# A two-layer trunk kernel: more seven-product pairs in layer 0, sums made by transfers, late loads on GpSimd's queue

## The chip, the cores and the metric

The kernel runs on one core of a Trainium2 chip. The metric is device time in microseconds (us) of one execution. A profiled execution gives the trace, in which the time of each instruction on each engine is recorded: TensorE (PE; its weight loads are PEld), VectorE (DVE), ScalarE (ACT), GpSimd (POOL) and SyncE (SP), which issues most transfers.

## What is computed

One step of a decoder of two layers for a prompt of 512 tokens and 8 samples of 8 tokens, 576 columns in all, model width 1024, inner width 2048:

```python
x = x + short_conv_mixer(rmsnorm(x))   # layer 0
x = x + mlstm_mixer(rmsnorm(x))        # layer 1, 4 heads of 512
y = rmsnorm(x)

def short_conv_mixer(h, buf, w_in, conv_w, w_out):
    b_gate, c_gate, xa, z = jnp.split(h @ w_in, 4, axis=-1)
    u = c_gate * xa
    conv, new_buf = causal_dwconv(u, buf, conv_w)
    y = b_gate * conv * jax.nn.silu(z)
    return y @ w_out, new_buf

def mlstm_mixer(...):
    xm, z = jnp.split(h @ w_in, 2, axis=-1)
    xc, new_buf = causal_dwconv(xm, conv_buf, conv_w)
    xc = jax.nn.silu(xc + conv_b)
    q, k, v = xc @ w_q, xc @ w_k, xm @ w_v
    ...   # gates, chunkwise matrix memory with state C, n, m for prompt and samples
    out = (norm(h) * onorm_w + skip * xc) * jax.nn.silu(z)
    return out @ w_out, new_buf, C, n, m
```

Everything is float32. A product of float32 matrices is made of three matmuls of rounded parts: high by high, high by low, low by high.

## The kernel before

**Tiles.** Tokens lie along the free axis (576 columns, two halves HT of 288), features along the 128 partitions. A weight chunk is 1024 x 128, loaded as one 512 KB tile `wr` of eight blocks of 128 x 128. There are four such raw buffers. ScalarE casts half a chunk (128x512) to the high part `wh` (L214, L263), VectorE subtracts for the low part `wl` (L215, L264). High and low parts have four buffers each.

**Layer 0** runs over f = 0 to 15 (L590 on). Each f needs the four chunks 4f to 4f+3: c, xa, z and b. A pair of chunks can be done in two ways. The plain one is two calls of `products` (L234), each 8 blocks x 3 parts x 2 column ranges (256 and 320). The other is `block_pair`: the chunks' eight blocks each are seen as a 2 x 2 block matrix, even blocks of the first chunk a11, odd ones a12, those of the second chunk a21 and a22, and the product with the 2 x 2 form of the activations is made from seven products in place of eight, each of four blocks x three parts on 288 columns (L332). The price is sums of weight blocks, made by VectorE: s1 = a21 + a22 (L297), s2 = s1 + a11 (L298), and inside the pair s2 += a12 and a21 += a11 (both L337). The pair's results are combined on ScalarE and VectorE (L342 to L384).

The pair (c, xa) of f+1 is done this way in every turn from f = 1 on. The pair (z, b) of f is done this way only if f is in `SECOND`, before the change 3, 5, 7, 9, 11 and 13. `block_weights` (L301) loads a pair's two chunks and makes s1 and s2 ahead of time, while the pair before is multiplied. s1, s2 and the pair's scratch `pu` are tiles of `X`, which has seven buffers; from f = 11 on c and xa lie there too. A copy of two columns per f is made by GpSimd (L602).

**Layer 1** has its input products in a loop over f (L684 on), where `xm` of some f is multiplied by VectorE straight out of PSUM and of others copied by ScalarE first. Then q and k of each (head h, tile dt) are made by pairs; `spread` (L742 to L748) repeats columns of k in a tile `kd`, which TensorE transposes (`tb`, L756).

**The late part** goes head by head and sample by sample. State tiles are loaded (c<-cs, L177), updated (c, L1222), stored (cs_out<-c, L1191). Values and keys of the prompt, written to memory earlier, come back by `fetch` (L1128): `kss` and `kps` keys, `vps` and `vss` values, `xcs`, `x1s` and `far`, all issued on SP's queue. Key stacks are scaled on ScalarE (L1122). The norm of a head needs `ln`: columns copied by GpSimd (L1315), VectorE's sums, a power on GpSimd (L1323), and VectorE again. `ns` (L1162) is a small sum on GpSimd per head stage.

**Order.** The program is written in one piece and a scheduler orders each engine's instructions by its own estimate of their times. An engine runs its instructions in that order, and an instruction whose input is late holds back all behind it on its engine. SP's transfers wait in the same way: for a free buffer, for data to store, or for a store whose buffer is to be loaded again.

Of the kernel before, what the change touches and what calls it, by code (L numbers as in the profile page):

```python
# [12 lines left out]
ALU = mybir.AluOpType  # L13
# [3 lines left out]
P = 128  # L17
# [3 lines left out]
NW = W // P  # L21
# [34 lines left out]
LAG = 6  # L56
AHEAD = 2
FH = 2
SECOND = tuple(range(3, 14, 2))
FI = 1  # L60
EARLY = 3.45
NEARLY = 10
# [5 lines left out]
def trunk(tc, io):  # L68
    nc = tc.nc
    ctx = ExitStack()  # L70
    with ctx:
# [34 lines left out]
        layer0 = [False]  # L106
# [37 lines left out]
        load = nc.sync.dma_start  # L144
        store = nc.sync.dma_start
        store_act = nc.scalar.dma_start

        cols = const.tile([P, NCOL], F32, name="cols")
        cst = const.tile([P, NCST], F32, name="cst")
# [150 lines left out]

        def block_weights(c1, c2, six=False):  # L301

            groups, behind = [], []
            for i in range(1 + six):
                r1, r2 = weight_tile(), weight_tile()
                for r, c_ in ((r1, c1 + i), (r2, c2 + i)):
                    latest[0] = load(out=r, in_=io["wts"][c_]).ins
                groups.append(block_sums(r1, r2, (8, 4)[i]))
                behind = [r1, r2] if i else []
            ahead_of[c1, c2] = groups, behind  # L310

        def block_pair(c1, c2, fs, xs, out1, out2, add, mid=None, then=None, pops=0, groups=None,
# [24 lines left out]
                    tt(g[out], g[out], g[block_], ALU.add)  # L337

            bx = block("p1")
            product(bx, a11, "b11", True)  # L340
            by = block("p6")
            nc.scalar.activation(by, bx, AF.Copy, scale=-1.0)  # L342
# [7 lines left out]
            nc.scalar.copy(u, by)  # L350
            add_up(s2, a12)
            product(bx, a12, "b21", False)
            add_up(a21, a11)
            run(pops)
            if pops:
                drip()
# [324 lines left out]
        for f in range(NW):  # L681
            if f % 4 == 0:
                ext = T(352, name="ext")
                load(out=ext, in_=io["exb"][f // 4])  # L684
            ext_f = ext[:, 88 * (f % 4):88 * (f % 4) + 88].rearrange("p (b t) -> p b t", t=11)
            if f < 2:
                u = raws[f]
                nc.vector.tensor_tensor(u, u, rb, ALU.mult)
            else:
                acc = gemm(80 + f, 1, h2)  # L690
                u = T(name="xm")
                if 3 < f < NW - 2:
                    nc.vector.tensor_tensor(u, flat(acc), rb, ALU.mult)
                else:
                    nc.scalar.copy(u, flat(acc))
                    nc.vector.tensor_tensor(u, u, rb, ALU.mult)
            us.append(u)
            if f >= 8:
                xm.append(split(u))
            elif f % 2:  # L700
                fm.append(forms(us[f - 1], u))

            cv = []

            def begin(f=f, u=u, ext_f=ext_f, cv=cv):
                cv.append(T(name="xc"))
                cv.extend(conv_steps(cv[0], u, ext_f, [col(f"cb{j}", f) for j in range(4)]))
                cv[1]()

            def end(f=f, u=u, ext=ext, cv=cv):  # L710
                nc.gpsimd.tensor_copy(cpb[:, f, :], u[:, NP - 3:NP])
                nc.scalar.activation(cv[0], cv[0], AF.Silu, bias=col("cbias", f))
                store_act(out=xcs[f], in_=cv[0])
                if f % 4 == 3:
                    store(out=io["exb_out"][f // 4], in_=ext)
                if f == NW - 1:
                    store(out=io["cpb_out"], in_=cpb)

            slow.extend([begin] + [lambda s=s, cv=cv: cv[s]() for s in (2, 3, 4)] + [end])
            if f >= LAG:  # L720
                for _ in range(5):
                    drip()
            if f == NW - 3:
                block_weights(96, 98)
# [14 lines left out]
                else:  # L739
                    nc.vector.tensor_tensor(gacc[:, a:b], g[:, 0:b - a], gacc[:, a:b], ALU.add)  # L740

        def spread(t, dup):  # L742

            for u in range(2):
                nc.gpsimd.tensor_copy(
                    dup[:, 128 * u:128 * u + 128].rearrange("p (g s t) -> p g s t", g=4, s=4),
                    t[:, NP + 32 * u:NP + 32 * u + 32].rearrange("p (g t) -> p g t", t=8)
                    .unsqueeze(2).broadcast_to([P, 4, 4, 8]))  # L748
# [155 lines left out]
        for h in (3, 0, 1, 2):  # L904
            st = heads[h]
            for dt in range(4):
                f = 4 * h + dt
                k, q = T(name="k"), T(name="q")

                def next_stage():  # L910
                    for m in range(KD):
                        x = T(name="x")
                        load(out=x, in_=x1s[m])
                        xs.append(x)
                    run(len(work))
                    second_norm(range(KD))

                if (h, dt) == (2, 3):
                    xs = []
                then = next(((128 + 4 * g, 130 + 4 * g, True) for i, g in enumerate(order) if i and order[i - 1] == f), None)  # L920
                if (h, dt) == (3, 0):
                    gemm_first(128 + 4 * f, 130 + 4 * f, fc, xc, k, q, [lambda j=j: mixed_load(j) for j in (4, 5)], then)
                else:
                    gemm_pair(128 + 4 * f, 130 + 4 * f, fc, xc[4:], k, q, mid=[next_stage] if (h, dt) == (2, 3) else None, then=then, pops=1)
                st["kt"].append(k)
                if dt % 2 == 0:
                    st["kd"].append(T(512, name="kd"))
                dup = st["kd"][-1][:, 256 * (dt % 2):256 * (dt % 2) + 256]
                spread(k, dup)
                if (h, dt) == (3, 0):  # L930
                    work.extend([lambda: None] * 2)
                work.append(lambda k=k, dup=dup, h=h, dt=dt: by_token(
                    k, dup, KSCALE, kps[h][dt].rearrange("p (i d) -> p i d", d=128),
                    kss[h][:, :, 128 * dt:128 * dt + 128]))
                last_q = last_act[0]
                st["qt"].append(q)
                if dt % 2 == 0:
                    qpt = T(512, name="qp")
                    nc.gpsimd.memset(qpt, 0.0)
                    st["qp"].append(qpt.rearrange("p (d x) -> p d x", d=2))  # L940
                query_norm(st, dt, q)
                for u in range(2):
                    nc.gpsimd.tensor_copy(
                        st["qp"][-1][:, dt % 2, 128 * u:128 * u + 128].rearrange("p (g x) -> p g x", x=32)[:, :, 8 * u:8 * u + 8],
                        q[:, NP + 32 * u:NP + 32 * u + 32].rearrange("p (g t) -> p g t", t=8))
# [182 lines left out]
        def fetch(name, *srcs, n=512):  # L1128

            fetched[name] = []  # L1130
            for src in srcs:
                t = T(n, name="ld")
                load(out=t, in_=src)
                fetched[name].append(t)

        def fetch_values(h):
# [473 lines left out]
def _arrays(a):  # L1610
# [5 lines left out]
    kq = np.stack([_chunks(f["b_w_k"][0]), _chunks(f["b_w_q"][0])], 1)  # L1616
    wts = np.concatenate([t.reshape(-1, P, KD, P) for t in (
        ain, _chunks(f["a_w_out"][0]), bin_[:NW], _chunks(f["b_w_v"][0]), kq, bin_[NW:], _chunks(f["b_w_out"][0]))], 0)
    cols = np.zeros((P, NCOL), np.float32)

    def put(name, v):
# [80 lines left out]
```

## Time and profile before

| | us |
|---|---|
| median of three runs (lowest, highest) | 1684.31 (1682.43, 1685.41) |
| the profiled execution | 1682.5 |
| its span, first to last instruction | 1680.7 |
| TensorE busy (matmuls) | 1648.2, 98% |
| VectorE busy | 1121.4, 67% |
| ScalarE busy | 781.2, 46% |
| GpSimd busy | 107.9, 6% |
| moved by transfers, mean | 166 GB/s |

The span is what the trace covers; the time of the execution is a little longer. Busy time of an engine leaves out what it issues and waits for. The granted clock of TensorE, 1.00 at full speed (2.4 GHz) and 0.50 at half (1.2 GHz), has a mean of 0.99.

### The profile page before, as it was taken

What the parts mean: (1) busy time and instruction counts of PE and PEld (TensorE: products, weight loads), DVE (VectorE), ACT (ScalarE), POOL (GpSimd) and SP (SyncE); (2) the same over time, 40 slices, a digit from 0 to 9 for tenths busy, and PEclk for the clock granted to TensorE, in tenths of its full rate; (3) what the DMA queues carried; (4) which work ended last, traced back from release to release, by engine and by line L of the source; (5) the groups of instructions that cost most, each with busy time, mean ns of one, the idle gap of its engine ahead of it and who ended that gap; (6) DMA issues with size and microseconds to landing.
All of it is one profiled execution on the core that took longest, in us unless ns stands there. A gap on an engine that the chain in (4) does not pass through costs nothing. (4 is left out here: it accounts for less than half of the span.)

```text
span 1680.7 us, 31096 instructions
## 1 busy us (share of the span) xinstructions
PE 1648.2 (98%) x12161; PEld 1569.9 (93%) x12161; DVE 1121.4 (67%) x2108; ACT 781.2 (46%) x1548; POOL 107.9 (6%) x241
## 2 busy tenths in 40 slices
PE   9999999999999999999899999999999998998998
PEld 9999999999999999999899989998988787988998
DVE  7988888874336975556856456456468567687775
ACT  5555555543224554535544334344345456555421
POOL 0000000000000000000211010101002000000000
PEclk9999999999999999999999999999999899999999
DMA  5233223333432434535434554453655687997982
GB/s 197 73 96 93 96 88 105 92 104 125 128 114 91 145 116 137 170 116 161 143 107 145 156 183 151 154 182 126 200 184 212 203 275 249 336 341 280 369 305 105
DMA packets 109794, 279.57 MB, mean 166 GB/s; under 512 B 11312, under 2 KB 33712, under 8 KB 109648
## 3 DMA queue, kind: packets, MB, share of 16 engines
q1 hardware_dynamic: 94288, 260.27, 47.2%
q10 hardware_dynamic: 15360, 17.32, 3.0%
q8 instruction: 95, 1.56, 0.4%
q14 instruction: 51, 0.42, 0.1%
HBM read 213.89 MB, written 63.66 MB: 165 GB/s over the span
## 5 line engine op out<-in xcount | busy, mean ns | idle before, releaser
L332 PE MATMUL p<-hi,wh 128*128 128x288 f32 x1316 | 389.3, 297 | 2.1 <-ACT p L342 1.5
L332 PE MATMUL p<-lo,wh 128*128 128x288 f32 x1316 | 387.6, 295 | 0.0
L332 PE MATMUL p<-hi,wl 128*128 128x288 f32 x1316 | 386.7, 295 | 0.0
L234 PE MATMUL acc<-hi,wh 128*128 128x256 f32 (+1 forms) x1328 | 288.9, 299 | 6.2 <-ACT num L1288 5.0
L234 PE MATMUL acc<-lo,wh 128*128 128x256 f32 (+1 forms) x1328 | 288.4, 297 | 0.0
L234 PE MATMUL acc<-hi,wl 128*128 128x256 f32 (+1 forms) x1328 | 287.1, 297 | 0.0
L332 PEld LDWEIGHTS p<-hi,wh 128*128 128x128 f32 x1316 | 247.3, 188 | 10.4 <-DVE ws L337 4.1
L263 ACT CAST wh<-wr 128x256 fp32r<-128x256 f32 (+1 forms) x266 | 152.0, 572 | 225.0 <-PE p L332 120.6
L332 PEld LDWEIGHTS p<-lo,wh 128*128 128x128 f32 x1316 | 247.7, 188 | 0.0
L332 PEld LDWEIGHTS p<-hi,wl 128*128 128x128 f32 x1316 | 247.0, 188 | 0.0
L214 ACT CAST wh<-wr 128x512 fp32r<-128x512 f32 x202 | 124.8, 620 | 239.3 <-PE acc L234 181.0
L234 PEld LDWEIGHTS acc<-hi,wh 128*128 128x128 f32 x1328 | 224.1, 190 | 11.7 <-ACT num L1288 5.2
L264 DVE TENSOR_TENSOR wl<-wr,wh 128x256 fp32r<-128x256 f32 (+1 forms) x266 | 163.1, 627 | 96.2 <-ACT wh L263 94.2
L234 PEld LDWEIGHTS acc<-hi,wl 128*128 128x128 f32 x1328 | 223.7, 190 | 1.5 <-issue 1.3
L234 PEld LDWEIGHTS acc<-lo,wh 128*128 128x128 f32 x1328 | 224.1, 190 | 0.5 <-issue 0.2
L215 DVE TENSOR_TENSOR wl<-wr,wh 128x512 fp32r<-128x512 f32 x202 | 138.7, 688 | 110.7 <-ACT wh L214 102.5
L263 ACT CAST wh<-ws 128x512 fp32r<-128x512 f32 (+1 forms) x177 | 99.9, 566 | 208.6 <-PE p L332 120.7
L264 DVE TENSOR_TENSOR wl<-ws,wh 128x512 fp32r<-128x512 f32 (+1 forms) x177 | 108.7, 620 | 57.6 <-ACT wh L263 57.5
L1222 DVE SCALAR_TENSOR_TENSOR c<-c,cols,r 128x512 f32<-128x512 f32 x128 | 91.3, 739 | 31.6 <-PE r L1221 26.2
L417 PE MATMUL p<-hi,wh 128*128 128x288 f32 x496 | 109.2, 300 | 0.0
L417 PE MATMUL p<-hi,wl 128*128 128x288 f32 x496 | 107.3, 295 | 0.0
L417 PE MATMUL p<-lo,wh 128*128 128x288 f32 x496 | 107.0, 295 | 0.0
(382 smaller groups left out, 2572.8 us busy)
## 6 DMA issues: line engine op xcount, KB each, us to landing
wr<-wts SPq DMA_DIRECT2D x222, 512.0 KB, 3.6
c<-cs SPq DMA_DIRECT2D x112, 512.0 KB, 5.9
cs_out<-c SPq DMA_DIRECT2D x64, 512.0 KB, 6.4
x<-xcs SPq DMA_DIRECT2D x20, 288.0 KB, 4.7
x<-xT SPq DMA_DIRECT2D x16, 288.0 KB, 4.2
xcs<-xc ACTq DMA_DIRECT2D x16, 288.0 KB, 2.5
ld<-xcs SPq DMA_DIRECT2D x16, 288.0 KB, 8.1
cp_out<-cp ACTq DMA_DIRECT2D x16, 257.0 KB, 7.0
```

The lines of the kernel that those rows point to most:

```text
L214: last_act[0] = nc.scalar.copy(hi, raw[:, 4 * i:4 * i + 4, :]).ins
L215: nc.vector.tensor_tensor(lo, raw[:, 4 * i:4 * i + 4, :], hi.bitcast(F32), ALU.subtract)
L234: nc.tensor.matmul(acc[:, o:o + j - i], a[:, k % 4, :], x[:, i:j], start=(first and k == 0 and p == 0), stop=(last and k == 7 and p == 2))
L263: last_act[0] = nc.scalar.copy(hi, src).ins
L264: nc.vector.tensor_tensor(lo, src, hi.bitcast(F32), ALU.subtract)
L332: nc.tensor.matmul(bank_, a[:, j, :], x, start=(start and n + j + i == 0), stop=(n == len(groups) - 1 and j == len(g) - 1 and i == 2), ski ...
L417: nc.tensor.matmul(b, a[:, k % 4, :], x[:, t:t + HT], start=bool(start) and k == 0 and i == 0, stop=(k == n - 1 and i == 2), skip_group_ch ...
L1222: ins = nc.vector.scalar_tensor_tensor(ct[:, j, :], ct[:, j, :], dec[:, o + j:o + j + 1], r, ALU.mult, ALU.add).ins
```

## The change

Five things change.

1. `SECOND` becomes 2 to 14: thirteen second pairs by seven products, six before.
2. In layer 0 the weights of the chunks that go by `block_pair` are written on the host with their even blocks first, so that a11, a12, a21 and a22 are contiguous halves. `block_weights` loads the two chunks, loads one half of the second chunk once more into s1, and issues two adding transfers on GpSimd's queue: the other half of that chunk onto s1, and the first half of the first chunk onto a21. VectorE makes s2 = s1 + a11 at the start of the pair and s2 += a12 inside it.
3. In layer 1 the product `xm` of f = 3 is multiplied by VectorE straight from PSUM.
4. The `spread` copies for (h, dt) = (3, 0) are made by ScalarE in place of GpSimd, and two empty items in the list of work are gone.
5. `fetch` issues on GpSimd's queue.

```diff
-SECOND = tuple(range(3, 14, 2))
+SECOND = tuple(range(2, 15))
...
+        add_load = nc.gpsimd.dma_start
...
         def block_weights(c1, c2, six=False):
 
+            if layer0[0]:
+
+                r1, r2 = weight_tile(), weight_tile()
+                for r, c_ in ((r1, c1), (r2, c2)):
+                    latest[0] = load(out=r, in_=io["wts"][c_]).ins
+                a11, a12, a21, a22 = [r[:, i:i + 4, :] for r in (r1, r2) for i in (0, 4)]
+                s1, s2 = [X(512, name="ws").rearrange("p (k x) -> p k x", x=P) for _ in range(2)]
+                load(out=s1, in_=io["wts"][c2][:, 0:4, :])
+                add_load(out=s1, in_=io["wts"][c2][:, 4:8, :], accum_op=ALU.add)
+                add_load(out=a21, in_=io["wts"][c1][:, 0:4, :], accum_op=ALU.add)
+                ahead_of[c1, c2] = [(a11, a12, a21, a22, s1, s2)], []
+                return
...
             bx = block("p1")
+            if layer0[0]:
+                tt(groups[0][s2], groups[0][s1], groups[0][a11], ALU.add)
             product(bx, a11, "b11", True)
...
-            add_up(a21, a11)
+            if not layer0[0]:
+                add_up(a21, a11)
...
-                if 3 < f < NW - 2:
+                if 2 < f < NW - 2:
                     nc.vector.tensor_tensor(u, flat(acc), rb, ALU.mult)
...
-        def spread(t, dup):
+        def spread(t, dup, copy=nc.gpsimd.tensor_copy):
...
-                nc.gpsimd.tensor_copy(
+                copy(
...
-                spread(k, dup)
-                if (h, dt) == (3, 0):
-                    work.extend([lambda: None] * 2)
+                spread(k, dup, *[nc.scalar.copy] * ((h, dt) == (3, 0)))
...
-                load(out=t, in_=src)
+                nc.gpsimd.dma_start(out=t, in_=src)
...
+    blk = [c for c in range(8, 64) if c % 4 < 2 or c // 4 in SECOND]
+    wts[blk] = wts[blk][:, :, [0, 2, 4, 6, 1, 3, 5, 7]]
```

How this moves instructions is shown at three places; lines of the changed kernel are 16 or so higher than those of the kernel before (L264 is L265 there, L337 is L350, L1133 is L1147, L1315 is L1329, L1323 is L1337). A row is line, operation, output and inputs with their buffers' numbers, and the tile's size.

VectorE in layer 0, over the second half of a pair: before, the next pair's sums stand among the splits `wl` of this one.

```order
L264 TENSOR_TENSOR wl_1862<-ws_1699,wh_1861 128x512
L297 TENSOR_TENSOR ws_1832<-wr_1829 128x512
L298 TENSOR_TENSOR ws_1833<-ws_1832,wr_1828 128x512
L337 TENSOR_TENSOR wr_1829<-wr_1829,wr_1828 128x4x128
L264 TENSOR_TENSOR wl_1882<-ws_1700,wh_1881 128x512
L337 TENSOR_TENSOR ws_1700<-ws_1700,wr_1695 128x512
```

In the changed kernel a whole pair reads so.

```order
L350 TENSOR_TENSOR ws_2025<-ws_2024,wr_2020 128x512
L265 TENSOR_TENSOR wl_2242<-wr_2020,wh_2241 128x512
L660 TENSOR_TENSOR z_2029<-z_2029,rb_470 128x576
L265 TENSOR_TENSOR wl_2260<-wr_2021,wh_2259 128x512
L662 TENSOR_TENSOR cv_1871<-b_2030,cv_1871 128x576
L265 TENSOR_TENSOR wl_2277<-ws_2025,wh_2276 128x512
L663 TENSOR_TENSOR cv_1871<-cv_1871,z_2029 128x576
L354 TENSOR_TENSOR ws_2173<-ws_2172,wr_2168 128x512
```

Two of four sums are left, and s2 of the next pair (L354) stands ahead of this pair's last split.

GpSimd in layer 0: before, one copy of two columns per f.

```order
L602 COPY cpa<-u_1550 128x2
L602 COPY cpa<-u_1826 128x2
L602 COPY cpa<-u_2120 128x2
L602 COPY cpa<-u_2396 128x2
L602 COPY cpa<-u_2693 128x2
```

After, the adding transfers stand between the copies, two for each pair, 27 pairs in all.

```order
L312 DMA ws_1728<-wts 128x512
L618 COPY cpa<-u_1574 128x2
L313 DMA wr_1725<-wts 128x512
L312 DMA ws_1876<-wts 128x512
L313 DMA wr_1873<-wts 128x512
L312 DMA ws_2024<-wts 128x512
L618 COPY cpa<-u_1870 128x2
L313 DMA wr_2021<-wts 128x512
```

The copies keep their order, and each now stands behind transfers that wait for the chunk or for the first half of s1.

GpSimd in the late part, from the norm of one head (copy of `qc`, power) to the next head's first copies: before, nothing stands between.

```order
L1315 COPY ln_18067<-qc_16793 128x1
L1323 TENSOR_TENSOR ln_18067<-ln_18067,half 128x5
L1162 TENSOR_TENSOR ns_19285<-nst,cols_15623 128x16
L1315 COPY ln_18730<-num_18535 128x1
L1315 COPY ln_18730<-num_18550 128x1
```

After, the fetches do.

```order
L1329 COPY ln_18219<-qc_16945 128x1
L1337 TENSOR_TENSOR ln_18219<-ln_18219,half 128x5
L1147 DMA ld_18356<-kps_7276 128x512
L1147 DMA ld_18358<-kps_7276 128x512
L1147 DMA ld_18479<-x1s 128x576
L1147 DMA ld_18481<-x1s 128x576
L1176 TENSOR_TENSOR ns_19437<-nst,cols_15775 128x16
L1147 DMA ld_18594<-x1s 128x576
L1147 DMA ld_18623<-kss_7284 128x512
L1329 COPY ln_18882<-num_18687 128x1
L1329 COPY ln_18882<-num_18702 128x1
```

The key fetch `kss` of this head stands right behind `ns` and one other fetch. At the first head six fetches stand between the copy of `qc` and the power.

## Rows read from the trace of the kernel before

**Rows 1.** The page's first part: busy us, share of the span, instructions.

```profile
PE 1648.2 (98%) x12161; PEld 1569.9 (93%) x12161; DVE 1121.4 (67%) x2108; ACT 781.2 (46%) x1548; POOL 107.9 (6%) x241
```

**Rows 2.** By stretch: length, busy PE, PEld, DVE, ACT, POOL, clock, DMA share, GB/s.

```profile
236.61:258.83 22.22, 22.22 (x170) 22.22 (x169) 18.37 (x32) 13.23 (x27) 0.59 (x1) 1.00 0.28 95
258.83:282.76 23.93, 23.93 (x183) 23.93 (x181) 20.71 (x36) 11.46 (x23) 0.59 (x1) 1.00 0.28 89
...
80.00:360.00 280.00, 280.00 (x2113) 280.00 (x2113) 237.41 (x410) 150.32 (x298) 7.61 (x13) 1.00 0.30 95
...
850.00:1260.00 410.00, 410.00 (x3053) 373.96 (x3052) 223.54 (x436) 174.45 (x368) 41.42 (x106) 1.00 0.51 160
1320.00:1580.00 260.00, 244.10 (x1656) 220.97 (x1657) 186.03 (x379) 139.69 (x298) 12.39 (x29) 0.95 0.86 295
```

**Rows 3.** Waits of TensorE: us in total, times, longest.

```profile
PE tb L756 <- POOL kd L745: 3.1, 1, 3.1
...
PE r L1221 <- DVE c L1222: 1.9, 7, 0.8
...
PE acc L234 <- ACT xm L695: 1.0, 1, 1.0
```

**Rows 4.** Single lines, 80 to 360 us: ns min/median/max; VectorE's wait at L297.

```profile
L297 DVE TENSOR_TENSOR ws<-wr x18: 678/692/695, 86.6 to 340.5; 128x512 f32<-128x512 f32 x18
...
  DMA wr<-wts: 7.7, 11
...
L602 POOL COPY cpa<-u x13: 583/586/587, 81.0 to 357.8; 128x2 f32<-128x2 f32 x13
```

**Rows 5.** Weight loads: KB each, median us to landing; 80 to 360, then 850 to 1260.

```profile
wr<-wts SPq DMA_DIRECT2D x49, 512.0 KB, 3.5
...
wr<-wts SPq DMA_DIRECT2D x55, 512.0 KB, 3.5
```

**Rows 6.** Timelines of SP and VectorE: start, us, engine, line, operation.

```profile
238.20 5.83 SPq L307 DMA_DIRECT2D wr<-wts  x2
...
253.48 0.69 DVE L264 TENSOR_TENSOR wl<-wr,wh 128x512 fp32r<-128x512 f32 x1
```

**Rows 7.** Around 830 us: timelines, the copies' ns min/median/max, two stretches by window.

```profile
829.42 7.50 POOL L745 COPY kd<-k 128x128 f32<-128x128 f32 x2 [23.19 <-issue]
836.86 0.52 POOL L939 MEMSET qp<- 128x512 f32 x1
...
L745 POOL COPY kd<-k x32: 288/737/7263, 829.4 to 1261.2; 128x128 f32<-128x128 f32 x32
...
837.34:840.75 3.41, 3.41 (x16) 3.41 (x15) 0.64 (x2) 1.07 (x3) 1.11 (x6) 0.50 0.00 0
834.00:836.70 2.70, 0.00 (x0) 0.00 (x0) 2.70 (x8) 0.05 (x1) 2.70 (x2) 1.00 0.56 124
```

**Rows 8.** Around 1545 us: SP's timeline, a wait of SP, the chain, TensorE, a stretch.

```profile
1535.11 0.34 SPq L1191 DMA_DIRECT2D cs_out<-c  x1
1542.36 0.33 SPq L177 DMA_DIRECT2D c<-cs  x1
...
1543.21 0.43 SPq L1133 DMA_DIRECT2D ld<-kss  x1
...
SPq L177 <- DMA cs_out<-c: 70.4, 35, 6.8
...
1543.21 5.79 DMA ld<-kss
...
1550.27 0.85 PE L234 MATMUL acc<-hi,wh 128*128 128x256 f32 x2 [5.00 <-ACT num L1288]
...
1547.30:1554.10 6.80, 3.83 (x16) 3.83 (x17) 3.85 (x11) 4.03 (x11) 0.37 (x2) 0.50 0.99 377
```

**Rows 9.** Timeline of GpSimd in the late part.

```profile
1348.91 1.56 POOL L1323 TENSOR_TENSOR ln<-ln,half 128x5 f32<-128x5 f32 x1 [4.84 <-DVE ln L1322]
...
1530.64 0.53 POOL L1162 TENSOR_TENSOR ns<-nst,cols 128x16 f32<-128x16 f32 x1 [16.73 <-DVE nst L1164]
```

## The prediction

> **What bounds the kernel now.** I read the page's busy shares first, then the busy times by stretch and the waits of TensorE, and after that single stalls in the timelines. TensorE is the bound: it is busy 1648.2 of 1680.7 us [rows 1], and over layer 0, from 80 to 360 us, for 280.00 of 280 us at full clock, while VectorE is busy 237 us of it, ScalarE 150 and GpSimd 8 [rows 2]. A change in layer 0 is thus worth what TensorE no longer has to do there, as long as nothing else comes to be late. All that TensorE waits for is short: the list of its waits has 5.0 us once, 3.1 once, 1.0 once at the places that the change touches [rows 3, 8]. The late stretch, from 1320 to 1580 us, is of another kind: TensorE is busy 244.10 of 260 us at a mean clock of 0.95 with the DMA engines at 0.86 [rows 2]. There a transfer that comes late is what ends a wait.
>
> The profiled execution took 1682.5 us and the median of the three runs is 1684.31, so I add up against 1682.5 and put 1.8 us on the result. A difference of 0.2%, some 3.4 us, is about what a measurement of this kernel can tell from no change.
>
> **Layer 0: seven more block pairs.** Second pairs go from 6 to 13. Two plain chunks are 2 x 8 x 3 x 2 = 96 matmuls, a block pair is 7 x 4 x 3 = 84, and both stream 288 columns on average. So 7 x 12 = 84 matmuls go. At 280.00 us / 2113 = 0.1325 us each [rows 2] that is 11.1 us. A second reading: one turn of the loop with two block pairs takes 22.22 us, the next one with a block pair and two plain chunks 23.93 [rows 2]; 1.71 x 7 = 12.0 us. I take 11.1, since the rows of the second reading differ by a few records that the trace has or lacks.
>
> What the pairs cost elsewhere: VectorE makes four sums of 128x512 per pair now, at 0.69 us each [rows 4], and 18.37 of 22.22 us are busy in a turn with two pairs [rows 2]. After the change two of the four are left (the order shows L354 and L350 only), so a turn of two pairs has about 18.4 - 4 x 0.69 = 15.6 us. VectorE gets lighter, also against a turn with plain chunks (20.71 of 23.93). ScalarE stays at some 13 of 22 us. Neither comes to be the bound.
>
> The price is transfers. A pair loaded 1.0 MB and now moves 1.75 MB, two of its transfers adding to what is in the buffer. Two pairs in 22.2 us make 158 GB/s, where some 95 flow now [rows 2]; between 850 and 1260 us 160 GB/s flow while TensorE is never idle, and the 512 KB loads land in the same 3.5 us there as in layer 0 [rows 2, 5]. So the amount alone is no trouble. The chain is: load half a chunk into s1 (SP), then add the other half (GpSimd), then VectorE makes s2. For the pair ahead of the one that starts at 258.83, two loads were issued from 238.20 on, over 5.83 us [rows 6]; the s1 load stands between them, so it is issued by 243.7 and lands by 247.2 with 3.5 us. If the adding transfer takes another 3.5 us, s1 is there at 250.7. In the new order VectorE wants it right ahead of the last split of the pair before, which stood at 253.48 [rows 6]: 2.8 us in hand. That split's matmuls start at 247.72 + 6/7 x 11.11 = 257.2 (the turn began at 236.61 and holds two pairs), so TensorE itself would stand only if s1 came after about 256.5, an adding transfer of over 9.3 us. No row of the trace shows an adding transfer. Bounds: 3.5 us, as a load of twice its size [rows 5], up to 3.5 + 7.26, if GpSimd has to wait for VectorE as one of its copies did (below). I take the lower end, since the other GpSimd work in layer 0, thirteen copies of two columns, takes 0.583 to 0.587 us each, without a slow one, though VectorE is busy 85% of the time [rows 2, 4].
>
> The Trainium skill speaks against this part. "SBUF — State Buffer", section "Who interferes with whom", says that a DMA issued by GpSimd has its descriptors written by that engine, which is locked out while VectorE runs in a mode that takes both port pairs, and advises to issue such transfers elsewhere. The same section keeps instructions with two inputs in SBUF apart from these: they hold up reads of GpSimd and no writes. The slow copy and the MEMSET of 0.52 us behind it agree with that; the trace has no descriptor writing. By the first the sum would be the slower rival's; by the second it stays.
>
> From the eleventh turn on c and xa lie in the seven scratch buffers that s1, s2 and the pair's own sums use too; there s1 can wait for a buffer. VectorE's splits run 256.5 - 253.4 = 3.1 us ahead, and three second pairs are added there, so up to 9 us; I take 1, because only a wait longer than that lead costs anything. Layer 0: -11.1 + 1 = -10, bounds -12 and -2.
>
> **The copies of (3, 0).** At 829.42 GpSimd made two copies of 128x128 that took 7.50 us together; VectorE had no gap in the last 2.70 us of it, and the MEMSET right behind took 0.52 [rows 7]. One of the two took 7.26 us; the median of all 32 is 0.74 [rows 7]. TensorE stood for 3.1 us [rows 3] and then ran until 840.75 at the half clock: matmuls 0.24 us apart, 3.41 us of them busy, of which 1.7 is the slowness [rows 7]. ScalarE makes the copies now. No row shows such a copy on it, but in the tail of the stall, from 834.00 to 836.70, it was busy for 0.05 of 2.70 us [rows 7]. So at best -3.1 - 1.7 = -4.8, at worst 0, if ScalarE's own casts come late by the two copies. I take -4. The two empty items that are dropped let the transposes come earlier in TensorE's order, so they want the copies earlier; the 0.8 us that I keep back are for that.
>
> **Layer 1, f = 3.** VectorE takes the product out of PSUM in place of a ScalarE copy and a multiplication. TensorE waited 1.0 us for that copy [rows 3]: -0.5, bounds -1 and 0.
>
> **Late fetches.** 81 loads go from SP's queue to GpSimd's. The one that costs most: SP issued nothing between 1535.11 and 1542.36, since its next issue, a load of c, waited for a store (6.8 us at the longest, over 1260 to 1681 us); the key fetch behind it went out at 1543.21 and took 5.79 us, and TensorE stood 5.00 us until 1550.27 [rows 8]. It had the half clock from 1547.30 to 1554.10, with 3.83 us busy in it, so another 1.9 us [rows 8]. On GpSimd the same fetch stands behind the small addition ns, which was done at 1531.17 [rows 9]. Even with 6 us to landing it would be there at 1538. So this stall goes: -6.9. What is next late? The DMA engines are 0.99 busy in that stretch at 377 GB/s [rows 8], so earlier fetches push stores and loads of c back, and TensorE waits for these elsewhere (r for c, 1.9 us in 7 [rows 3]). I give back 2.9 and take -4.
>
> Against it stands GpSimd's own order. Ahead of head 0's power, which ran at 1348.91, there are now six fetches; an issue took SP 0.33 to 0.43 us, and the power waited 4.84 us for VectorE anyway [rows 8, 9], which covers them at up to 0.8 us each. In return fetches stand behind copies and ns that wait for ScalarE and VectorE, once 16.73 us [rows 9]. So the other bound is a new stall like the old one, +5; the term lies between -7 and +5.
>
> The rule in "DMA: Bandwidth & Descriptors", section "Issuing engines are not separate DMA queues", is that moving an issue to another engine saves no more than the issuing engine's time. The row of SP's silence shows more than issue time, a fetch that stands behind another issue's wait. By the rule this term is 0; that is the first rival.
>
> **Sum.** -10 - 4 - 0.5 - 4 = -18.5, so 1664.0 for a profiled execution and 1666 for the median.
>
> **The rivals.** First: the late fetches change nothing, since transfers end when the DMA engines let them. For it: 0.86 busy over 260 us. Against it: SP's silence at 1535. Then -14.5: 1670; with 3 to 5 us lost on GpSimd, up to 1675. Second: s1 comes late only where scratch buffers are short, and ScalarE's copies push its casts: -11.1 + 9 and nothing for (3, 0), nothing late; some -2, so 1682. For it: seven buffers for more users. Against it: the lead of 3.1 us. Third, slower: GpSimd's adding transfers start when VectorE lets them. With 7.26 us of waiting and 3.5 of moving, s1 comes at 258.0, 1.5 us after the point at which TensorE stands, and there are 27 pairs: +40 on -18.5 makes about 1706. It decides from an adding transfer of 9.3 us on. For it: the copy of 7.26 us. Against it: thirteen copies in layer 0 at 0.585 us.
>
> **How the numbers follow.** Forecast 1666 with a chance of 0.48; first rival 0.29; second 0.12; third 0.11. The bounds of the terms add to -12 - 4.8 - 1 - 7 = -25 at the one end, 1659.5, a little lower if the stalls of the clock in the late stretch shrink too. The upper end takes in the first rival and most of the second: 1684. Outside are the third and a little at the lower end: 1657 to 1684. Faster by over 3.4 us, below 1681: 0.48 + 0.29 + a third of the second, 0.81; within it 0.08; slower 0.11.
>
> **What would show it.** Right: a turn of layer 0 with two pairs at 22.2 us from the second to the fourteenth, TensorE's idle time there still 0; 84 matmuls fewer; no wait of tb at about 820 us and a full clock there; the key fetch of the last head issued before SP's load of c and no 5 us gap of the q product near 1535. Wrong: a wait for ws or DMA in VectorE's list in layer 0 longer than its 7.7 us now [rows 4], turns longer than 22.3 us, or TensorE's waits in the late stretch as long in sum as before, under other names.

## The result and the profile after

The changed kernel takes 1673.29 us (median of five runs, 1670.57 to 1677.22) beside 1684.31 before (1682.43 to 1686.54): a ratio of 0.9943, 95% interval 0.9929 to 0.9956, 11 us less. In a second set it took 1673.93 beside 1682.55 (0.9950, 0.9934 to 0.9966). Faster was forecast, and the time lies in the range of 1657 to 1684, but 7 us above the 1666 forecast: 11 us of some 18 came, which is the first rival's time.

The page of the profile after, first part and transfers by queue (packets, MB, share of the 16 engines), to be read beside [rows 1]:

```profile
PE 1641.0 (98%) x12077; PEld 1561.9 (93%) x12077; DVE 1122.7 (67%) x2117; ACT 806.2 (48%) x1612; POOL 191.8 (11%) x374
...
q1 hardware_dynamic: 86512, 245.33, 44.7%
q0 software_dynamic: 14256, 36.18, 9.3%
```

TensorE has 12161 - 12077 = 84 matmuls less. The queue of GpSimd, q0, is new.

By stretch (length; busy PE, PEld, DVE, ACT, POOL; clock; DMA share; GB/s), one turn of layer 0 with two pairs, then most of layer 0, then three pieces around 1310 us, in the changed kernel:

```profile
197.25:219.49 22.24, 22.24 (x170) 22.24 (x169) 19.41 (x35) 14.11 (x31) 3.85 (x5) 1.00 0.73 177
80.00:350.00 270.00, 270.00 (x2042) 270.00 (x2041) 236.77 (x415) 171.07 (x352) 46.96 (x61) 1.00 0.69 168
1290.00:1307.77 17.77, 17.77 (x107) 11.83 (x105) 6.44 (x10) 6.98 (x13) 2.23 (x4) 1.00 0.47 148
1307.77:1324.83 17.06, 17.06 (x58) 13.56 (x58) 10.32 (x18) 7.26 (x16) 0.38 (x2) 0.50 0.57 170
1324.83:1340.00 15.17, 15.17 (x109) 12.30 (x109) 8.57 (x27) 5.35 (x13) 5.56 (x11) 1.00 0.67 228
```

A turn with two pairs takes 22.24 us, as the turn of 22.22 in [rows 2], and TensorE has no idle time in layer 0. Around 1310 us it is busy all the time too, but 17.06 us of that at the half clock.

TensorE's waits from 1240 to 1580 us in the changed kernel (in total, times, longest), to be read beside [rows 3]:

```profile
PE cp L1289 <- DVE lo L1280: 3.0, 3, 2.1
PE ha L1368 <- ACT y L1370: 2.9, 1, 2.9
PE r L1235 <- DVE c L1236: 2.6, 8, 0.8
PE pn L1174 <- DVE kst L1138: 2.1, 2, 1.5
PE acc L235 <- DVE qc L1316: 1.7, 2, 1.3
```

The 5.0 us in front of the output product are gone from the list, and so are the 3.1 us for the copies of (3, 0) from that of the whole kernel.

**Where the time went.** The late part runs nearly the same instructions in both kernels, in a somewhat different order, so the start of the matmul that has as many matmuls behind it can be compared between two traces. The table gives that shift against the trace of before, in us (the median over the matmuls of the 20 us ahead of the time of before named; a trace is one execution). The last two columns are read in each trace by itself: the time from 1200 to 1600 us at the half clock, and the sum of TensorE's listed waits from 1240 to 1640 us. "No fetch" is short for the fetches left on SP.

| kernel | 540 | 860 | 1300 | 1400 | 1540 | 1640 | half clock | waits |
|---|---|---|---|---|---|---|---|---|
| before | 0 | 0 | 0 | 0 | 0 | 0 | 27.3 | 16.6 |
| changed, first trace | -11.6 | -15.5 | -15.4 | -10.9 | -3.0 | -9.3 | 37.5 | 16.0 |
| changed, second trace (e9) | -11.7 | -15.7 | -15.7 | -12.6 | -7.0 | -13.3 | 27.3 | 16.9 |
| layer 0 alone (e1) | -12.0 | -10.9 | -10.7 | -8.8 | -6.6 | -12.9 | 27.3 | 13.7 |
| fetches alone (e2) | 0.2 | 0.0 | 0.0 | 3.6 | 8.3 | 3.5 | 37.5 | 15.5 |
| no fetch (e3) | -12.2 | -16.5 | -16.5 | -15.7 | -12.5 | -13.2 | 27.3 | 18.2 |
| no fetch, again (e10) | -12.3 | -14.6 | -14.6 | -14.1 | -10.8 | -15.2 | 23.9 | 16.0 |
| sums on VectorE (e4) | -10.8 | -11.2 | -11.0 | -6.9 | -5.0 | -11.3 | 30.7 | 13.2 |
| copies of (3, 0) alone (e5) | 0.5 | -3.3 | -3.2 | -1.8 | -2.5 | -2.4 | 30.7 | 15.2 |
| key fetch on GpSimd (e6) | -11.4 | -15.5 | -15.4 | -11.1 | -10.6 | -17.2 | 27.3 | 13.0 |
| key fetch, again (e11) | -11.4 | -15.4 | -15.4 | -14.4 | -13.0 | -17.7 | 23.9 | 12.9 |
| all but the key fetch (e12) | -11.5 | -13.2 | -13.1 | -10.3 | -10.3 | -15.5 | 23.9 | 13.5 |
| twelve pairs (e7) | -9.9 | -10.4 | -10.4 | -6.2 | -5.4 | -11.5 | 27.3 | 13.6 |

The traced execution need not be a typical one: that of e9 is the shortest of its six, those of e1, e2, e4 and e12 are the longest of theirs.

The changed kernel stands at -15.4 us at 1300 us, where the terms up to there add to -14.5: layer 0 and the copies of (3, 0) are in. So the whole miss lies behind 1300 us. It can be taken apart between equal matmuls, from the one at 1300.12 us of before to the one at 1540.10 and on to the one at 1640.05 (by stretch, as above; before, the changed kernel's first trace, e3):

```profile
1300.12:1540.10 239.98, 229.55 (x1553) 203.84 (x1552) 168.58 (x330) 134.48 (x286) 10.85 (x26) 0.96 0.81 278
1540.10:1640.05 99.95, 94.48 (x673) 91.18 (x672) 71.47 (x136) 35.85 (x72) 1.76 (x4) 0.97 0.91 327
```

```profile
1284.58:1537.74 253.16, 238.24 (x1553) 210.75 (x1552) 169.56 (x331) 135.03 (x286) 39.76 (x81) 0.93 0.78 267
1537.74:1630.77 93.03, 92.54 (x674) 89.46 (x672) 70.33 (x135) 35.89 (x72) 8.97 (x17) 1.00 0.94 343
```

```profile
1283.64:1528.00 244.36, 231.37 (x1553) 205.23 (x1552) 169.10 (x331) 135.07 (x286) 10.16 (x26) 0.95 0.80 273
1528.00:1626.89 98.89, 94.28 (x673) 90.92 (x672) 71.01 (x135) 35.84 (x72) 1.75 (x4) 0.98 0.93 333
```

In the first stretch the changed kernel takes 13.2 us more than before: TensorE is busy 8.7 us longer over the same matmuls, at a lower mean clock, and idle 4.5 us longer. In the second, where before stood for 5.0 us, it gets 6.9 back.

### The profile page after: what moved, and what is told of

Its sections match the earlier page's. It is cut to its first block, busy times and chain, and to the rows that moved or that the text cites. A ratio compares the mean times of both kernels' runs of the same rounds, so it can differ in the third digit from the quotient of the medians.

```text
span 1671.5 us, 31276 instructions
## 1 busy us (share of the span) xinstructions
PE 1641.0 (98%) x12077; PEld 1561.9 (93%) x12077; DVE 1122.7 (67%) x2117; ACT 806.2 (48%) x1612; POOL 191.8 (11%) x374
## 5 line engine op out<-in xcount | busy, mean ns | idle before, releaser
L345 PE MATMUL p<-hi,wh 128*128 128x288 f32 x1512 | 446.0, 297 | 2.1 <-ACT p L357 1.4
L345 PE MATMUL p<-lo,wh 128*128 128x288 f32 x1512 | 444.4, 295 | 0.0
L345 PE MATMUL p<-hi,wl 128*128 128x288 f32 x1512 | 442.7, 295 | 0.0
L345 PEld LDWEIGHTS p<-hi,wh 128*128 128x128 f32 x1512 | 283.3, 188 | 10.4 <-DVE ws L350 4.1
L264 ACT CAST wh<-wr 128x512 fp32r<-128x512 f32 (+1 forms) x294 | 169.1, 577 | 214.9 <-PE p L345 123.1
L265 DVE TENSOR_TENSOR wl<-wr,wh 128x512 fp32r<-128x512 f32 (+1 forms) x294 | 181.6, 633 | 95.8 <-ACT wh L264 93.7
L235 PE MATMUL acc<-hi,wh 128*128 128x256 f32 (+1 forms) x1104 | 241.1, 299 | 3.7 <-DVE qc L1316 1.7
L235 PE MATMUL acc<-hi,wl 128*128 128x256 f32 (+1 forms) x1104 | 240.8, 298 | 0.0
L235 PE MATMUL acc<-lo,wh 128*128 128x256 f32 (+1 forms) x1104 | 239.4, 298 | 0.0
L264 ACT CAST wh<-ws 128x512 fp32r<-128x512 f32 x198 | 113.0, 572 | 201.9 <-PE p L345 130.7
L235 PEld LDWEIGHTS acc<-hi,wh 128*128 128x128 f32 x1104 | 186.6, 191 | 9.4 <-DVE qc L1316 2.3
L235 PEld LDWEIGHTS acc<-hi,wl 128*128 128x128 f32 x1104 | 186.5, 191 | 1.7 <-issue 1.3
L235 PEld LDWEIGHTS acc<-lo,wh 128*128 128x128 f32 x1104 | 186.2, 191 | 0.6 <-issue 0.2
L265 DVE TENSOR_TENSOR wl<-ws,wh 128x512 fp32r<-128x512 f32 x198 | 123.2, 628 | 67.9 <-ACT wh L264 67.3
L433 PE MATMUL p<-hi,wh 128*128 128x288 f32 x496 | 109.2, 300 | 0.0
L433 PE MATMUL p<-hi,wl 128*128 128x288 f32 x496 | 107.3, 295 | 0.0
L433 PE MATMUL p<-lo,wh 128*128 128x288 f32 x496 | 107.0, 295 | 0.0
```

The costliest lines, as they stand in the source:

```text
L235: nc.tensor.matmul(acc[:, o:o + j - i], a[:, k % 4, :], x[:, i:j], start=(first and k == 0 and p == 0), stop=(last and k == 7 and p == 2))
L264: last_act[0] = nc.scalar.copy(hi, src).ins
L265: nc.vector.tensor_tensor(lo, src, hi.bitcast(F32), ALU.subtract)
L345: nc.tensor.matmul(bank_, a[:, j, :], x, start=(start and n + j + i == 0), stop=(n == len(groups) - 1 and j == len(g) - 1 and i == 2), ski ...
L433: nc.tensor.matmul(b, a[:, k % 4, :], x[:, t:t + HT], start=bool(start) and k == 0 and i == 0, stop=(k == n - 1 and i == 2), skip_group_ch ...
```

## The experiments

**Layer 0 alone and the fetches alone.** Theory A: the fetches on GpSimd's queue take the late time. Theory B: anything that comes earlier, or in another order, makes the late part fall differently. e1 keeps these edits and leaves the others out:

```diff
-SECOND = tuple(range(3, 14, 2))
+SECOND = tuple(range(2, 15))
...
+            if layer0[0]:
...
+                add_load(out=s1, in_=io["wts"][c2][:, 4:8, :], accum_op=ALU.add)
```

> Layer 0's part alone: thirteen second pairs and the adding transfers; the copies of (3, 0), f = 3 and the fetches as before. Theory A (the late loss comes from the fetches on GpSimd's queue): layer 0 takes 11.6 us and nothing is lost later, some 1673 us. Theory B (whatever makes the late part come 11 to 16 us earlier changes how its stalls and half-clock stretches fall, whoever issues the fetches): 5 to 6 us are lost again after 1300 us, some 1678.

e1 took 1668.95 us (1668.24 to 1670.18) beside 1684.09: 0.9917, 0.9899 to 0.9935. By the medians layer 0 alone gives 4 us more than the whole change, though the intervals overlap. The late part lost nothing in the end but gained 2.2 us from 1300 to 1640, so neither theory had it right. The stall near 1545 us of before is gone in e1, though its fetches are on SP's queue. SP's timeline in e1:

```profile
1529.31 0.34 SPq L1207 DMA_DIRECT2D cs_out<-c  x1
1532.22 0.33 SPq L178 DMA_DIRECT2D c<-cs  x1
1532.60 0.42 SPq L1149 DMA_DIRECT2D ld<-kss  x1
1533.12 0.38 SPq L1207 DMA_DIRECT2D cs_out<-c  x1
```

In [rows 8] the load of c waited until 1542.36 for a store that had been issued at 1535.11, 7.25 us; here it waited for one issued at 1529.31, 2.91 us, and the key fetch went out at 1532.60. The edits of e1 touch nothing in the late part, but they changed what the scheduler reckons: counted in the traces, 62 rows of SP's last 200 issues and 96 of VectorE's last 500 instructions differ from before's (a moved row counts twice). That the order is what removed the stall doesn't follow, as e3 shows below.

e2 makes the fetches' edit alone:

```diff
-                load(out=t, in_=src)
+                nc.gpsimd.dma_start(out=t, in_=src)
```

> The fetches on GpSimd's queue alone, all else as before. Theory A: the late part gets 6 us longer, some 1690 us, although the 5 us stall near 1545 us goes. Theory B: that stall goes and little else changes, 1678 to 1684 us, as the prediction's term of -4 has it.

1685.05 us (1678.63 to 1686.67) beside 1684.09: 1.0003, 0.9989 to 1.0018. No difference, neither the 6 us of theory A nor the 4 us of the prediction. The trace, of the longest of ten executions, shows both halves: up to 1540 us it loses 8.3 us, with 37.5 us at the half clock in place of 27.3, then it gets the old stall back, 4.8 us.

**The change without its fetches.** e3 is the changed kernel with

```diff
-                nc.gpsimd.dma_start(out=t, in_=src)
+                load(out=t, in_=src)
```

> The whole change but for the fetches, which SP issues as before. Theory A: layer 0's 11.6 us and the 4.0 us of (3, 0) stay to the end: 1668 to 1669 us. Theory B: the late part loses as much as in the changed kernel, 1673 us, or more, since the 5 us stall near 1545 us is back, 1677.

1669.84 us (1666.07 to 1671.94): 0.9919, 0.9893 to 0.9946. That is 3.4 us below the changed kernel by the medians, as theory A has it, though the intervals overlap. Yet its trace loses 3.3 us after 1300 us with no fetch on GpSimd. The old stall is back in it: SP's timeline and TensorE's wait, then the same wait in e10, the same kernel run again.

```profile
1524.20 0.38 SPq L1205 DMA_DIRECT2D cs_out<-c  x1
1530.39 0.33 SPq L178 DMA_DIRECT2D c<-cs  x1
1530.77 0.42 SPq L1147 DMA_DIRECT2D ld<-kss  x1
...
PE acc L235 <- ACT num L1302: 4.1, 1, 4.1
```

```profile
PE acc L235 <- ACT num L1302: 2.0, 1, 2.0
```

From some 845 us on every engine has the same instructions in the same order in the traces of e1, e3 and e10, and the stall is 0, 4.1 and 2.0 us. What differs is how long the load of c waits for the store ahead of it: 2.91, 6.19 and 5.54 us from the store's issue. So it is the time of that store, and not the order alone, that makes the stall. Why the store took so differently long isn't shown.

**Sums on VectorE.** e4 is the changed kernel without adding transfers: `block_weights` and `block_pair` as before, the weights in their old order, thirteen pairs.

> The whole change, but VectorE makes all four sums of a pair in layer 0 again and no transfer adds. Theory of the prediction (VectorE has room: 18.4 of 22.2 us busy in a turn with two pairs): TensorE does not stand in layer 0 and the time is that of the changed kernel, 1672 to 1675 us. Rival: with two pairs in every turn the splits come late somewhere, and TensorE stands in layer 0 for 3 us or more: 1676 to 1685 us.

1671.61 us (1668.05 to 1672.64): 0.9928, 0.9907 to 0.9949. The adding transfers are worth nothing that shows here. One turn with two pairs and layer 0 in e4:

```profile
188.53:210.78 22.25, 22.25 (x170) 22.25 (x169) 21.59 (x39) 14.02 (x31) 0.58 (x1) 1.00 0.33 103
80.00:350.00 270.00, 270.00 (x2042) 270.00 (x2041) 262.29 (x461) 170.38 (x352) 6.62 (x12) 1.00 0.31 99
```

VectorE is busy 21.59 of 22.25 us, and TensorE is still never idle. So the seven pairs were to be had without the transfers, with 0.7 us of room in a turn; with the transfers it is 2.8 us. The prediction gave the transfers no gain but room on VectorE, and this bears it out.

**The copies of (3, 0) alone.** e5 is before with the edit of `spread` alone, and the scheduler's late order is line by line that of before.

```diff
-                spread(k, dup)
-                if (h, dt) == (3, 0):
-                    work.extend([lambda: None] * 2)
+                spread(k, dup, *[nc.scalar.copy] * ((h, dt) == (3, 0)))
```

> The copies of (3, 0) on ScalarE alone, all else as before; the order of every engine in the late part is the same as before. Theory A (a gain ahead of the late part stays, as long as its order is the same): -4.0 us to the end, 1680 us. Theory B (the late part takes back what comes earlier, since its transfers set its end): 1683 to 1685 us, with the 4 us seen at 860 us and gone at 1560.

1679.36 us (1675.75 to 1680.50) beside 1681.29: 0.9981, 0.9969 to 0.9992. That is 1.3 to 5.2 us, which takes in theory A's 4.0 and hardly theory B. The trace has -3.9 us between 820 and 860 us and 0.8 us lost again after 1300, where a stretch at the half clock took 13.65 us in place of 10.24. Lines in the changed kernel that show the cause gone (duration ns min/median/max; then TensorE's timeline):

```profile
L761 ACT COPY kd<-k x2: 293/293/293, 821.5 to 821.7; 128x128 f32<-128x128 f32 x2
...
821.99 0.38 PE L772 MATMUL tb<-cst,kd 128*128 128x128 f32 x2
```

Two copies of 0.29 us on ScalarE are where [rows 7] had 7.50 us on GpSimd, and the transpose does not wait.

**One fetch.** e6 is the changed kernel with the key stacks alone on GpSimd's queue:

```diff
-                nc.gpsimd.dma_start(out=t, in_=src)
+                (nc.gpsimd.dma_start if name[0] == "ks" else load)(out=t, in_=src)
```

> The whole change, but of the fetches only the key stacks (kss) on GpSimd's queue, the rest on SP's. Theory A (the key fetch behind a blocked load of c costs 4 to 5 us, and the other fetches on GpSimd cost what they cost): the stall near 1537 us goes, 1664 to 1667 us. Theory B (the late part's length follows how its order falls, not one queue): anywhere from 1667 to 1674 us.

1665.59 us (1663.17 to 1666.48) beside 1681.29: 0.9896, 0.9877 to 0.9915. It met theory A's number. Whether the theory holds was left to the last set.

**Twelve pairs.** e7 is e1 with `SECOND = tuple(range(3, 15))`.

> Layer 0's part alone with twelve second pairs (3 to 14) in place of thirteen: 12 matmuls more, 1.6 us. Theory A: 1.6 us more than with thirteen alone, 1670.5 us. Theory B: the late order differs from that of the thirteen, and the late part differs by several us either way, whatever the 1.6.

1671.77 us (1670.10 to 1674.18) beside 1681.29: 0.9938, 0.9914 to 0.9962. Beside e1's ratio that is 0.0021, 3.5 us, with intervals that overlap: the 1.6 us can neither be read nor denied. In the traces layer 0 is 2.1 us longer than e1's, and the late part differs by some 1 us, though 68 rows of VectorE's last 500 differ from before's.

**The room of the adding transfers.** e8 is e1 with the adding transfer onto s1 three times (s1 then holds three times that half). It was run once.

```diff
                 add_load(out=s1, in_=io["wts"][c2][:, 4:8, :], accum_op=ALU.add)
+                add_load(out=s1, in_=io["wts"][c2][:, 4:8, :], accum_op=ALU.add)
+                add_load(out=s1, in_=io["wts"][c2][:, 4:8, :], accum_op=ALU.add)
```

> Layer 0's part alone, with the adding transfer onto s1 made three times (so s1 holds three times that half, and the output is not the reference's). The chain of the prediction (s1 may come 9.3 us after its first half has landed before TensorE stands; the adding transfers took 4.9 us): two more put s1 some 5 us too late in each of 27 pairs, +100 us or more in layer 0. Rival: the adding transfers are issued further ahead than the chain has it, and layer 0 stays at its length, within 5 us.

1781.46 us. The first 620 us of e8 and the same number of matmuls in e1, by window, then TensorE's and VectorE's waits from 80 to 450 us in e8, then the adding transfers (KB, median us to landing) in e8 and in the changed kernel:

```profile
0.00:620.00 620.00, 535.73 (x3796) 526.79 (x3797) 373.35 (x655) 269.26 (x522) 108.91 (x138) 0.93 0.60 148
0.00:508.50 508.50, 504.66 (x3796) 502.36 (x3797) 375.44 (x655) 270.61 (x522) 61.24 (x84) 1.00 0.56 153
...
PE p L347 <- DVE wl L265: 57.3, 14, 7.6
...
DVE ws L356 <- DMA ws<-wts: 100.3, 19, 8.7
...
ws<-wts POOLq DMA_DIRECT2D x70, 256.0 KB, 5.2
```

```profile
ws<-wts POOLq DMA_DIRECT2D x24, 256.0 KB, 4.9
wr<-wts POOLq DMA_DIRECT2D x24, 256.0 KB, 4.2
ws<-wts SPq DMA_DIRECT2D x23, 256.0 KB, 4.3
```

VectorE waits 100 us for s1 and TensorE for VectorE's splits. Layer 0 ends 99.5 us later than in before, 111.5 later than in e1: TensorE is idle for 84.27 us in place of 3.84, some 80 more or 3.0 a pair, and busy for 31 us longer over the same 3796 matmuls, with a mean clock of 0.93 in place of 1.00. Three transfers of 5.2 us are 15.6, so as an estimate TensorE begins to stand at some 15.6 - 3.0 = 12.6 us of adding, where the prediction had 9.3; the point itself was not measured. That a late s1 stops TensorE is shown, and one adding transfer of 4.9 us lies far inside.

**The last set, all beside each other.** e9 is the changed kernel, e10 is e3, e11 is e6, and e12 turns e6's choice round: all fetches on GpSimd but the key stacks.

```diff
-                nc.gpsimd.dma_start(out=t, in_=src)
+                (load if name[0] == "ks" else nc.gpsimd.dma_start)(out=t, in_=src)
```

> The changed kernel itself, timed beside the next three: 1673 us. Half-clock time between 1200 and 1600 us 37.5 us, as in its first trace; if the length of its late part were chance of one execution, both would come out elsewhere.

> The change with all fetches on SP's queue, again: 1667 to 1670 us, faster than the changed kernel by 3 to 4 us (theory: all fetches on GpSimd's queue cost that much in the late part). If the queue made no difference: within 1 us of it.

> The change with the key stacks alone on GpSimd's queue, again: 1664 to 1667 us, 3 to 4 us below the one with all on SP's (theory: the key fetch no longer stands behind a load of c that waits, and nothing else is moved). If the 4 us between the two was scatter between calls: the same time, 1667 to 1670.

> The change with all fetches but the key stacks on GpSimd's queue. Theory (the key fetch gains 4 us, the others lose 7): the loss without the gain, 1676 to 1678 us, the stall ahead of the output product near 1535 us back and half-clock time of 34 us or more. Rival (each new order of the late part falls as it falls): anywhere from 1665 to 1675.

| kernel | median us (range) | ratio to before, 1682.55 | 95% interval |
|---|---|---|---|
| changed (e9) | 1673.93 (1669.26 to 1676.69) | 0.9950 | 0.9934 to 0.9966 |
| all fetches on SP (e10) | 1666.74 (1663.43 to 1673.35) | 0.9909 | 0.9889 to 0.9929 |
| key stacks on GpSimd (e11) | 1665.80 (1664.31 to 1668.47) | 0.9899 | 0.9884 to 0.9915 |
| all but the key stacks (e12) | 1665.76 (1661.84 to 1667.03) | 0.9893 | 0.9876 to 0.9910 |

The theory of a key fetch that gains 4 us and others that lose 7 falls: with exactly the others on GpSimd, e12 is as fast as e11. Nor is e11 3 to 4 us below e10. The intervals of the last three overlap, and none overlaps with the changed kernel's, if narrowly for e10. So in this set all fetches on GpSimd cost 7 to 8 us beside the three other sharings of them; beside e3 it was 3.4 us with intervals that overlap, and next to nothing when the rest of the change is left out (e2).

e9's time came out as expected and its time at the half clock did not. Its trace adds a thing: the same program, two executions, 1671.5 and 1667.5 us of span. The pieces around 1310 us in e9, to be put beside those of the first trace above:

```profile
1290.00:1310.28 20.28, 20.28 (x118) 13.50 (x117) 6.87 (x11) 8.73 (x17) 2.23 (x4) 1.00 0.47 168
1310.28:1320.52 10.24, 10.24 (x36) 8.37 (x37) 8.44 (x15) 4.69 (x11) 0.19 (x1) 0.50 0.62 170
1320.52:1340.00 19.48, 19.48 (x144) 16.53 (x142) 12.22 (x35) 7.77 (x17) 5.74 (x12) 1.00 0.59 198
```

10.24 us at the half clock where it was 17.06 before, with the same order and TensorE busy throughout in both. Over 1200 to 1600 us it is 27.3 and 37.5 us; half of the difference is 5.1 us, about the 4.0 us between the spans. Over all executions of the last set the mean granted clock is 0.9883 for the changed kernel and 0.9905, 0.9918 and 0.9914 for e10, e11 and e12. On a span of 1670 us that is, as an estimate, 4 to 6 of the 7 to 8 us.

## Why the prediction was right or wrong

**Layer 0, right.** -10 was forecast, -11.6 came, and -10.8 to -12.3 in the eight other traces with these thirteen pairs (e8 aside). The count of 84 matmuls at 0.1325 us gave 11.1, the difference of two turns 12.0. The 1 us for scratch buffers was not needed: TensorE is busy 270.00 of 270 us.

**The cost on VectorE, mis-sized without effect.** The 15.6 us of a turn are 19.41. I took 18.37 us from one turn that has two pairs [rows 2], but the turns before shared work unevenly: 18.37 and 20.71 have a mean of 19.5, and e4 with four sums in every pair needs 21.59. A turn that follows another kind of turn is not the steady state. So VectorE did not get lighter: 236.77 of 270 us are 0.88, where 237.41 of 280 were 0.85 [rows 2].

**The adding transfers, right in kind.** They took 4.9 and 4.2 us in place of the 3.5 assumed, and TensorE did not wait. By the Trainium skill, "SBUF — State Buffer", section "Who interferes with whom", a transfer issued on GpSimd can be held up while VectorE is in a mode that takes both port pairs. With VectorE busy 236.77 of 270 us, nearly all of it in instructions with two inputs, 256 KB took 4.2 to 4.9 us from GpSimd and 4.3 from SP: no run here shows the delay.

**The copies of (3, 0), right at their place.** -4 forecast, -4.0 in the trace of the changed kernel and -3.9 in that of e5 between 820 and 860 us. e10 and e12 have the same edit and no wait of `tb`, but 3.41 us at the half clock near 813 us, and gained 2.4 and 1.8. At the end the term can't be told: e1 lacks it and took 1668.95 us, e3 has it and took 1669.84.

**f = 3, wrong, and small.** TensorE's wait of 1.0 us for `xm` is still in the changed kernel's list (PE acc L235 <- ACT xm L711, 1.0 us once). It stands on the copy of f = 2, which stays on ScalarE, so the term is 0 and not -0.5: I had the line of the wait right and the turn of the loop wrong.

**Late fetches, wrong.** -4 was forecast, within -7 to +5. Alone they changed nothing (e2, 1.0003), and in the whole change they cost 3.4 us by e3 and 7 by e10. The step "so this stall goes: -6.9" came true: no trace with the key fetch on GpSimd has the stall (the changed kernel twice, e2, e4, e6, e11), and from 1540.10 us of before on the changed kernel takes 93.03 us where before took 99.95, 6.9 less. The fetch went out earlier, as the timeline of GpSimd in the changed kernel shows:

```profile
1527.43 0.21 POOL L1176 TENSOR_TENSOR ns<-nst,cols 128x16 f32<-128x16 f32 x1 [13.16 <-DVE nst L1178]
1528.05 0.57 POOL L1147 DMA_DIRECT2D ld<-x1s  x1 [0.41 <-POOL ns L1176]
1528.68 0.55 POOL L1147 DMA_DIRECT2D ld<-kss  x1
```

The step that failed is "I give back 2.9", the price of what is next late. From 1300.12 to 1540.10 us of before the changed kernel lost 13.2 us in its first trace and 9.4 in its second, e2 10.3. Part of this comes without any fetch on GpSimd: e1, e3 and e10 lost 4.2 to 4.5 us there. Beside e3 the changed kernel lost 8.8 us there in its first trace and 5.0 in the second, its shortest execution, and got 5.9 back behind it. I had read the new order for one fetch and given the rest of the late part a share of a stall's length.

The gain was less certain than I had it, too. With the key fetch on SP the stall was 5.0 us in before, 4.2 in e5, 4.1 in e3, 3.8 in e8, 2.0 in e10, and absent or 0.2 in e1, e7 and e12. A stall whose length changes between executions of one order is a poor term of a sum.

What the loss is made of is shown. Of the 8.8 us beside e3 TensorE is busy 6.9 longer over the same 1553 matmuls, with the clock at a mean of 0.93 in place of 0.95, and idle 1.9 longer. In the prediction's sum the half clock stands only behind single stalls; that it would hold longer in the rest of the late part was put at nothing, without a reason. Why all fetches on GpSimd bring more of it than most of them or one stays open. The amount of reordering doesn't tell: of TensorE's last 2000 matmuls 358 rows differ from before's in the changed kernel and 382 in e12, which is fast. A test with one order of all engines and the queue alone changed was not made, since the order follows from the scheduler.

One sign of being wrong that the prediction names came true: TensorE's waits in the late stretch are as long in sum as before, under other names, 16.0 us and 16.6.

**The rival of the rule.** The rule of the Trainium skill in "DMA: Bandwidth & Descriptors", section "Issuing engines are not separate DMA queues", gives the issuing engine no influence beyond its issue time. e2, at 1.0003, agrees with it; e9 beside e10 to e12 does not, unless the changed order is taken for the cause, which fits with the rule. My first rival, 1670 to 1675 us, is where the time came out: the late fetches gained nothing in sum. Its reason holds only in sum, since the stall did go and the loss came elsewhere. That the time still fell in the stated range is owed to this rival, and not to the term as forecast.

**The slower rivals.** Neither came. e8 shows the end of the third's chain, that a late s1 stops TensorE, by the estimate from 12.6 us of adding on; the change stays some 8 us away from it. That VectorE holds GpSimd's transfers back, with which that rival begins, no run shows.

**The better version.** Without its fetches, or with either part of them, the change takes 1665.8 to 1666.7 us in the last set (1665.59 and 1669.84 in e6 and e3), below both kernels. That is the 1666 forecast, for another kernel, and by luck: the terms that make it up there are others.

## What to carry to other kernels

- On a stretch where the bound engine is never idle, count its instructions: 84 matmuls at their own rate were 11.1 us, and 10.8 to 12.3 came. In a stretch that ends on transfers, read a stall in more than one trace before it becomes a term of a sum: under one and the same order it was 0, 2.0 and 4.1 us here.
- Run each part of a bundle alone. Here one part gave as much alone as all five together or more, and the one that spoiled the sum was neutral alone.
- Before moving sums from an engine to transfers, try whether the engine has room for them: here it had, by 0.7 us in 22.

## What the runs showed of the hardware

- A half clock without idle time. From 1307.77 to 1324.83 us TensorE is busy for 17.06 of 17.06 us at 0.50; in the stretch ahead of it it was busy for 17.77 of 17.77 us at 1.00. In this earlier stretch it ran 107 matmuls with 11.83 us of weight loads; a turn of layer 0, at the full clock throughout, has 170 with 22.24 in 22.24 us. The length of such a stretch differed between two executions of one program, 17.06 and 10.24 us.
- A GpSimd issue of a 256 KB fetch took 0.54 us in the late part, one of an adding transfer in layer 0 0.86, where SP took 0.33 to 0.43 [rows 8]. An adding transfer of 256 KB landed 4.2 to 4.9 us after its issue, a plain one of SP after 4.3, at 168 GB/s in all.
- One store of 512 KB held SP's queue for very different times under one order of instructions: the load of c behind it was issued 2.91 us (e1), 6.19 (e3) and 5.54 (e10) after the store, and 7.25 us in before [rows 8].
- In the late part the fetches on GpSimd landed later than the same on SP in e3, for the 288 KB ones: median 9.9 beside 7.2 us for `xcs`, 9.6 beside 7.0 for `x1s`; the key stacks 5.8 beside 6.2. The queue isn't shown to be the cause: the stores `cp_out`, which ScalarE issues in both, took 8.8 beside 6.9. The lists by queue, from 1310 to 1570 us, in the changed kernel and then in e3:

```profile
ld<-xcs POOLq DMA_DIRECT2D x16, 288.0 KB, 9.9
cp_out<-cp ACTq DMA_DIRECT2D x16, 257.0 KB, 8.8
...
ld<-x1s POOLq DMA_DIRECT2D x8, 288.0 KB, 9.6
ld<-kss POOLq DMA_DIRECT2D x6, 256.0 KB, 5.8
```

```profile
ld<-xcs SPq DMA_DIRECT2D x16, 288.0 KB, 7.2
cp_out<-cp ACTq DMA_DIRECT2D x16, 257.0 KB, 6.9
...
ld<-x1s SPq DMA_DIRECT2D x6, 288.0 KB, 7.0
ld<-kss SPq DMA_DIRECT2D x6, 256.0 KB, 6.2
```
